# Softmax normalisation and square sums moved to GpSimd, queries split once with DMAs to place the halves, in a one-core hybrid attention and FFN block

## The chip, the core and the metric

The kernel runs on one core of a Trainium2 chip. The metric is the device time of one execution in microseconds (us), lower is better. TensorE (PE) multiplies; VectorE (DVE), ScalarE (ACT) and GpSimd (POOL) work elementwise; SyncE (SP) issues the DMAs. Each engine works through its own queue in program order, and waits on semaphores for what other engines produce.

## The reference

One layer over 512 tokens of width 2048, in fp32, cut to what matters here:

```
h    = rms_norm(x)                       # over 2048 channels: a sum of squares per token
proj = h @ w_in                          # 30 tiles of 128 columns: a q,k,v  b u,g  c q,k,v
out_a = dilated_mixture(rms(aq), rms(ak), av)      # 8 heads x 64, mixture of 3 windows
out_b = silu(layer_norm(causal_conv31(bu * sigmoid(bg))))   # 512 channels
out_c = band_attention(rms(cq), rms(ck), cv, sinks)         # 16 heads x 64, window 128
x = x + concat(out_a, out_b, out_c) @ w_out
h2 = rms_norm(x)                         # the second sum of squares
x = x + (silu(h2 @ w_gate) * (h2 @ w_up)) @ w_down          # d_ff 5632
```

In the attention, scores are shifted by their maximum, exponentiated, and divided by their sum. That division is one of the things that the change touches.

## The kernel before, in words

All arrays are held channels by tokens: a tile has 128 channels on the partitions and 512 tokens along the row. For precision every operand is split into a rounded high part (`hi`, type fp32r) and the remainder (`lo`), and each product is three matmuls, hi·hi, hi·lo and lo·hi (`mm3`, lines 248 to 251). A weight unit of 128x1024 is loaded by SP (L213), rounded by ACT (L226 or L231) and its remainder taken by DVE (L227 or L232). L232 takes the high part from a copy in PSUM, L227 from SBUF. Units are split two ahead of their use.

**Head (about 0 to 52 us).** x is loaded, scaled and split (`scaled`, L338 on ACT and L339 on DVE), and multiplied with the first four column tiles. Beside it `add_square` squares each x tile on ACT (L347) and adds it to `ssum` on DVE (L348). `token_scale` sums `ssum` over the partitions with matmuls (L289).

**Projection and attention (about 52 to 525 us).** `project` makes one tile of 128 columns from two weight units. A clock of ticks (`Ticks`, line 82) is advanced after every six matmuls. Everything else is put into the program at a set number of ticks after the tile it depends on, so the order on every engine is fixed by these numbers. After a q tile (two heads of 64 channels), `do_q` copies it to SBUF (`raw`, L471), then in the next tick takes the high part on ACT (L509), one tick later the remainder on DVE (L514), per head. For head h, the tile `q[h]` has the high part on that head's 64 partitions and the remainder on the other 64; the keys stand in both halves, so that one matmul of 128 partitions sums both products. Beside these, each of the 124 taps of the convolution (L424, L426, DVE) has a tick, and so have the keys (`do_k`, whose halves are copied across by two DMAs on SP, L546) and the values.

`attention` handles each head in units of one or two blocks of 128 queries: `scores` (PE, L615 and L616), `top` (DVE, L622: mask and maximum, reading PSUM), `exps` (ACT, L635), `norm` (DVE: the sums, L644 or L647, reciprocal, L649, and the division, L651, one instruction for each block of queries), `flip` (PE transposes of the normalised weights, L667), their split (`ph`, ACT L673; `pl`, DVE L678), `weigh` (PE, L691 and L692), and the output (`mix`, ACT L700 and DVE L705), which is split for the output projection at L736 and L737.

**Output projection (about 421 to 622 us).** Two halves of 16 units each. In the second half `residual` adds the product to x (L830, DVE), stores it, calls `add_square` for `ssum2`, and after every second tile `h2_of` makes the seven operands of a Strassen-like FFN product: two scalings on ACT (L812), four differences on DVE (L817 to L820), seven splits (L805 on ACT, L806 on DVE). From unit 88 on GpSimd adds weight blocks for the FFN (L178).

**FFN (about 622 us to the end).** Blocks of seven products each (L921). Its first block waits for `h2_of` and, for the second norm, for `ssum2`.

All 128x512 work tiles come from one pool of 75 slots, returned when the last user is done.

Of the kernel before, what the change touches and what calls it, by code (L numbers as in the profile page):

```python
# [9 lines left out]
F32 = mybir.dt.float32  # L10
F32R = mybir.dt.float32r
I32 = mybir.dt.int32
AF = mybir.ActivationFunctionType
ALU = mybir.AluOpType
# [7 lines left out]
HALF = (slice(0, HD), slice(HD, 2 * HD))  # L22
# [91 lines left out]
def kernel(ctx: ExitStack, tc: tile.TileContext, xT, wi, wo, wgu, wd, cst_in, outT):  # L114
    nc = tc.nc
# [16 lines left out]
    ticks = Ticks()  # L132

    def slot(name, dt=F32, cols=T):
        return sp.tile([P, cols], dt, name=name, tag="s")
# [203 lines left out]
        nc.vector.scalar_tensor_tensor(lo, x, g, hi.bitcast(F32), op0=ALU.mult, op1=ALU.subtract)  # L339
        return hi, lo  # L340

    def add_square(acc, x, k, tag):
        if k == 0:
            nc.scalar.activation(acc, x, AF.Square)
        else:
            sq = slot(f"{tag}{k}")
            nc.scalar.activation(sq, x, AF.Square)  # L347
            nc.vector.tensor_add(acc, acc, sq)  # L348

    def token_scale(acc, n, name, b=None):  # L350

# [9 lines left out]
    for k in range(2):  # L361
        h_hl[k] = scaled(xs[k], col(C_G1 + k), "h", k)
        split_up_to(k)
    pump(RAW_EARLY)
    add_square(ssum, xs[0], 0, "sq")
    for k in range(KT):
        if k < 2 or k % 2 == 0:
            wh, wl = next_unit()
            o = 0
        if k + X_AHEAD < KT:  # L370
            load_first(k + X_AHEAD)
        if k + 2 < KT:
            h_hl[k + 2] = scaled(xs[k + 2], col(C_G1 + k + 2), "h", k + 2)
        if k + 1 < KT:
            add_square(ssum, xs[k + 1], k + 1, "sq")
        hi, lo = h_hl.pop(k)
        h_hi.append(hi)
        h_lo.append(lo)
        for j in range(HEAD4):
            mm3(g4[j], wh[:, o:o + P], wl[:, o:o + P], hi, lo, k == 0, k == KT - 1)  # L380
            o += P
# [26 lines left out]
    hconv, yconv = {}, {}  # L408
# [22 lines left out]
    ln = {}  # L431
# [19 lines left out]
    def ln_square():  # L451
        ln["s"] = slot("lnv")
        for j in range(NB):
            add_square(ln["s"], yconv[j], j, "lq")

    def ln_var():
        ln["r"] = token_scale(ln.pop("s"), 512, "lv")[1]
# [10 lines left out]
    def head_scales(b, name, then):  # L468

        raw = slot(name + "raw")  # L470
        nc.scalar.copy(raw, b)  # L471

        def flip():
            b2 = bank(name + "f")
            for i in range(NT):
                nc.tensor.transpose(b2[:, i * P:(i + 1) * P], raw[:, i * P:(i + 1) * P], ident)
            ticks.after(1, square, b2)

        def square(b2):
            sq = slot(name + "sq")  # L480
            nc.scalar.activation(sq, b2, AF.Square)
            ticks.after(1, total, sq)

        def total(sq):
            v = cp.tile([P, NT, 2], F32, name=name + "v", tag="hsv", bufs=3)
            nc.vector.tensor_reduce(v.rearrange("p a b -> p (a b)"), sq.rearrange("p (a b) -> p a b", b=HD),
                                    axis=mybir.AxisListType.X, op=ALU.add)
            nc.vector.tensor_add(v, v, c64[:, :, None].to_broadcast([P, NT, 2]))
            ticks.after(1, power, v)

        def power(v):
            r = cp.tile([P, NT, 2], F32, name=name + "r", tag="hsr", bufs=4)
            nc.gpsimd.tensor_tensor(r, v, nhalf.rearrange("p (a b) -> p a b", b=2), op=ALU.pow)
            then(r)

        ticks.after(SQ, flip)
        return raw

    def do_q(box, b, name):
        def then(r):  # L500
            box["rq"] = r

        raw = head_scales(b, name, then)
        box["q at"] = ticks.now + SQ + 4
        q = box["q"] = [slot(f"{name}{h}", F32R) for h in range(2)]

        def high():
            for h in range(2):
                nc.scalar.copy(q[h][HALF[h]], raw[HALF[h]])  # L509
            ticks.after(1, low)  # L510

        def low():
            for h in range(2):
                nc.vector.tensor_sub(q[h][HALF[1 - h]], raw[HALF[h]], q[h][HALF[h]].bitcast(F32))  # L514
        ticks.after(1, high)

    def do_k(box, b, name, gi):
# [77 lines left out]
    def attention(kind, box, mix, mi, heads):  # L595
        ready, every, step, s1, sx, s2, fl, ev, we = C_TICKS if kind == "c" else A_TICKS
        name = mi
# [5 lines left out]
        def head(h):  # L603
            es = {}
            d = cp.tile([P, 4, NT], F32, name=f"{name}d{h}", tag="soft", bufs=6)
            mx, nm, den, rd = (d[:, i] for i in range(4))
# [33 lines left out]
            def norm(u):  # L640
                e = es[u]
                s = slice(us[u][0][0], us[u][-1][0] + 1)
                if kind == "c":
                    nc.vector.tensor_add(den[:, s], den[:, s], mx[:, s])  # L644
                else:
                    for i, k0, n, o in us[u]:
                        nc.vector.scalar_tensor_tensor(e[:, o:o + n], e[:, o:o + n], 1.0, mult_a[:, T - n:],  # L647
                                                       op0=ALU.mult, op1=ALU.mult, accum_out=den[:, i:i + 1])
                nc.vector.reciprocal(rd[:, s], den[:, s])  # L649
                for i, k0, n, o in us[u]:  # L650
                    nc.vector.tensor_scalar(e[:, o:o + n], e[:, o:o + n], rd[:, i:i + 1], None, op0=ALU.mult)  # L651

            ph, pl = {}, {}

# [21 lines left out]
            def low(t, b, o):  # L676
                pl[t] = slot(f"{name}pl{h}{t}", F32R)
                nc.vector.tensor_sub(pl[t][:, :o], b[:, :o], ph[t][:, :o].bitcast(F32))  # L678
# [36 lines left out]
            for u in range(len(us)):  # L715
                tu = t0 + u * step
                ticks.after(tu, scores, u)
                ticks.after(tu + s1, top, u)
                ticks.after(tu + s1 + sx, exps, u)
                ticks.after(tu + s1 + sx + s2, norm, u)  # L720
# [28 lines left out]
    ticks.after(t_ln + 2, ln_mean)  # L749
    ticks.after(t_ln + 4, ln_center)  # L750
    ticks.after(t_ln + 6, ln_square)
    ticks.after(t_ln + 9, ln_var)
    ticks.after(t_ln + 12, ln_out, mix)
# [4 lines left out]
    for name in PROJ[HEAD4:]:  # L758
        kind, what, j = name[0], name[1], name[2:]
        if name == PROJ[-1]:  # L760
            for n, row in enumerate(ROWS[:2]):
                ticks.after(4 + n, split_mix, row)
        b = project(name)
        if kind == "b":
            part[what + j] = b
            if what == "g":
                ticks.after(0, glu, int(j), part.pop("u" + j), part.pop("g" + j))
            continue
        if kind == "c":
            box = Heads(shared) if j else shared  # L770
        else:
            box = boxes.setdefault(j, {})
        if what == "k":
            do_k(box, b, name, 1 if kind == "c" else 0)
        elif what == "v":
            do_v(box, b, name)
        else:
            do_q(box, b, name)
        if what == "q":
            if kind == "a":  # L780
                boxes.pop(j)
            attention(kind, box, mix, kind + j, (int(j), int(j) + 8) if kind == "c" else None)
# [61 lines left out]
    for half in range(2):  # L844
        for i, n in enumerate(OUT_ORDER[half]):
# [6 lines left out]
            for kk in range(8):  # L852
                k = 8 * half + kk
# [4 lines left out]
                s = slice(kk * P, (kk + 1) * P)  # L858
# [221 lines left out]
    for g in range(2 * NP + len(DOWN)):  # L1080
# [5 lines left out]
        else:  # L1086
            n, first, end = DOWN[t]
# [116 lines left out]
```

## Time and profile before

| | before |
|---|---|
| median of 3 runs | 1931.52 us (1931.4 to 1932.05) |
| the profiled execution: span from first to last instruction | 1932.4 us |
| mean granted TensorE clock | 0.993 |
| busy, us: PE / DVE / ACT / POOL | 1899.8 / 1474.8 / 1334.0 / 993.4 |
| moved by DMA | 313.99 MB, mean 162 GB/s |

The profiled execution has no time of its own outside its span; its span stands 0.9 us above the median. How to read the rows that follow: a line number is one of the kernel's. `out<-in xcount` names tiles without buffer numbers. In the groups, "busy, mean ns" is followed by the engine's idle time before the instructions and by what ended it. In a table of windows, each row gives the stretch, its length, and the busy time (and count of instructions) of PE, PEld, DVE, ACT and POOL, then the granted clock of TensorE as a share of full speed, the DMA share and GB/s. In a timeline, the columns are start, duration, engine, line, operation, tiles, shape and count, and in brackets the idle time before it and what ended it.

### The profile page before, as it was taken

The numbers are of one execution on the slowest core, as the hardware profiler recorded it, in microseconds if no ns is written. First come the engines' busy times: TensorE is split into PE (matmuls) and PEld (weight loads), VectorE is DVE, ScalarE is ACT, GpSimd is POOL, SyncE is SP. The second block draws the span as 40 slices with busy tenths as digits, with TensorE's granted clock in tenths as the row PEclk, the third lists the DMA queues.
The fourth block names the chain that finished last, engine by engine and source line by source line (L and its number), as shares of the span: only waits on it lengthen the run. The fifth ranks groups of instructions, "written<-read, shape, count | busy, mean of one in ns | idle before, by whom it ended". The sixth has DMA issues, their size and how long they took to land.

```text
span 1932.4 us, 29509 instructions
## 1 busy us (share of the span) xinstructions
PE 1899.8 (98%) x10332; PEld 1645.2 (85%) x10332; DVE 1474.8 (76%) x2574; ACT 1334.0 (69%) x1848; POOL 993.4 (51%) x640
## 2 busy tenths in 40 slices
PE   8999999999999999999999999999999899999999
PEld 7888788778877888888888888888888788888888
DVE  6789988997468677777777777777777677767776
ACT  6355655553355788888887888888888677667675
POOL 0111011000001688877877888778887566656564
PEclk9999999989999899999999999999999999999999
DMA  7222222223332254535443444444447777777685
GB/s 263 75 99 72 66 88 77 72 87 113 122 114 93 94 184 139 174 126 178 150 167 133 165 164 159 141 159 167 159 142 259 286 275 278 269 243 272 202 276 195
DMA packets 132133, 313.99 MB, mean 162 GB/s; under 512 B 14736, under 2 KB 30224, under 8 KB 131984
## 3 DMA queue, kind: packets, MB, share of 16 engines
q1 hardware_dynamic: 131840, 312.01, 47.4%
q8 instruction: 81, 1.33, 0.3%
q14 instruction: 68, 0.56, 0.1%
q10 hardware_dynamic: 144, 0.10, 0.0%
HBM read 255.42 MB, written 55.31 MB: 161 GB/s over the span
## 4 chain that ended last, share of the span: by engine, by line
PE 70%; DMA 1%; DVE 0%; POOL 0%; ACT 0%; issue 0%; POOLq 0%; DVEq 0%
PE out L921 66%; PE o L250 1%; PE o L249 1%; PE o L251 1%; DMA w('22', 'd1')_15059<-in_wd 0%; DMA a<-od 0%; POOL w('21', 'd1')_15057 L178 0%; DVE xr L830 0%; PE out L289 0%; DVE h L806 0%; ACT sr L347 0%; ACT h L812 0%; DVE wl L232 0%; POOL w('s', 'd1')_15138 L178 0%; ACT wh L231 0%
## 5 line engine op out<-in xcount | busy, mean ns | idle before, releaser
L921 PE MATMUL out<-h,wh 128*128 128x512 f32 x2464 | 591.0, 392 | 3.6 <-DVE h L806 3.6
L921 PEld LDWEIGHTS out<-h,wh 128*128 128x128 f32 x2464 | 454.1, 189 | 91.8 <-DVE h L806 4.0
L921 PEld LDWEIGHTS out<-h,wl 128*128 128x128 f32 x2464 | 317.5, 192 | 13.8 <-ACT r2b L885 1.2
L921 PE MATMUL out<-h,wl 128*128 128x256 f32 x2464 | 321.5, 283 | 1.2 <-ACT r2b L885 0.9
L921 PE MATMUL out<-a,wh 128*128 128x512 f32 x1232 | 297.8, 392 | 4.2 <-DMA a<-od 3.0
L921 PEld LDWEIGHTS out<-a,wh 128*128 128x128 f32 x1232 | 226.0, 188 | 50.1 <-DMA a<-od 5.3
L921 PEld LDWEIGHTS out<-a,wl 128*128 128x128 f32 x1232 | 160.4, 193 | 8.1 <-DMA a<-od 1.5
L226 ACT CAST wh<-w 128x1024 fp32r<-128x1024 f32 (+1 forms) x93 | 96.8, 1040 | 99.4 <-PE o L250 33.2
L921 PE MATMUL out<-a,wl 128*128 128x256 f32 x1232 | 163.0, 284 | 0.9 <-DMA a<-od 0.9
L227 DVE TENSOR_TENSOR wl<-w,wh 128x1024 fp32r<-128x1024 f32 (+1 forms) x93 | 112.5, 1211 | 65.5 <-ACT wh L226 65.3
L934 DVE TENSOR_TENSOR y<-y,out 128x256 f32<-128x256 f32 x120 | 50.6, 421 | 64.0 <-PE out L921 60.9
L426 DVE SCALAR_TENSOR_TENSOR y<-bu,cst,y 128x511 f32<-128x511 f32 (+14 forms) x120 | 87.7, 731 | 0.7
L178 POOL TENSOR_TENSOR w('s', 'g1')_5639<-w('21', 'g1')_5403,w('22', 'g1')_5439 128x1024 f32<-128x1024 f32 x1 | 2.4, 2409 | 116.2 <-DVE wl L227 116.2
L935 DVE TENSOR_TENSOR y<-y,out 128x256 f32<-128x256 f32 x120 | 50.5, 421 | 4.1
L250 PE MATMUL o<-ml_c,wh 128*128 128x512 f32 x128 | 51.0, 398 | 2.1 <-DVE ml_c L737 2.1
L249 PE MATMUL cq<-hh,wh 128*128 128x512 f32 x128 | 51.3, 401 | 1.4 <-DVE mix_c L705 1.4
L249 PE MATMUL o<-mh_c,wh 128*128 128x512 f32 x128 | 51.7, 404 | 0.0
L251 PE MATMUL o<-mh_c,wl 128*128 128x512 f32 x128 | 50.7, 396 | 0.0
L251 PE MATMUL cq<-hh,wl 128*128 128x512 f32 x128 | 50.0, 390 | 0.0
L250 PE MATMUL cq<-hl,wh 128*128 128x512 f32 x128 | 49.9, 390 | 0.0
L249 PE MATMUL in<-hh,wh 128*128 128x512 f32 x64 | 26.3, 411 | 5.6 <-ACT wh L226 5.6
L250 PEld LDWEIGHTS o<-ml_c,wh 128*128 128x128 f32 x128 | 24.5, 191 | 7.5 <-DVE ml_c L737 3.1
(3093 smaller groups left out, 4835.4 us busy)
## 6 DMA issues: line engine op xcount, KB each, us to landing
a<-od SPq DMA_DIRECT2D x182, 256.0 KB, 5.3
od<-a SPq DMA_DIRECT2D x147, 256.0 KB, 3.8
w<-in_wi SPq DMA_DIRECT2D x59, 512.0 KB, 3.6
w<-in_wo SPq DMA_DIRECT2D x32, 512.0 KB, 3.6
y<-x2d SPq DMA_DIRECT2D x48, 256.0 KB, 5.3
x2d<-y SPq DMA_DIRECT2D x64, 128.0 KB, 3.3
x<-in_xT SPq DMA_DIRECT2D x16, 256.0 KB, 7.2
xr<-in_xT SPq DMA_DIRECT2D x16, 256.0 KB, 3.8
```

What stands on the lines that cost most here:

```text
L178: nc.gpsimd.tensor_add(out[:, :n], raws[key[a]][0][:, :n], raws[key[b]][0][:, :n])
L226: nc.scalar.copy(hi[:, :n], t[:, :n])
L227: eng.tensor_sub(lo[:, :n], t[:, :n], hi[:, :n].bitcast(F32))
L249: nc.tensor.matmul(out, wh, xh, start=start, stop=False)
L250: nc.tensor.matmul(out, wh, xl, start=False, stop=False)
L251: nc.tensor.matmul(out, wl, xh, start=False, stop=stop)
L426: nc.vector.scalar_tensor_tensor(yconv[j][:, i:], hconv[j][:, :T - i], c, yconv[j][:, i:], op0=ALU.mult, op1=ALU.add)
L921: nc.tensor.matmul(out, lhs[:, s], rhs, start=begin, stop=last and low == flip[0] and x is xs[-1], skip_group_check=True)
L934: sign(out, out if first is None else first, main)
L935: sign(out, out, rest)
```

## The change

Three edits, with nothing else moved.

```diff
-    def add_square(acc, x, k, tag):
+    def add_square(acc, x, k, tag, eng=nc.gpsimd):
         if k == 0:
             nc.scalar.activation(acc, x, AF.Square)
         else:
             sq = slot(f"{tag}{k}")
             nc.scalar.activation(sq, x, AF.Square)
-            nc.vector.tensor_add(acc, acc, sq)
+            eng.tensor_add(acc, acc, sq)
...
     def ln_square():
         ln["s"] = slot("lnv")
         for j in range(NB):
-            add_square(ln["s"], yconv[j], j, "lq")
+            add_square(ln["s"], yconv[j], j, "lq", nc.vector)
...
         def high():
+            hi = slot(f"{name}hi", F32R)
+            nc.scalar.copy(hi, raw)
+            ticks.after(1, low, hi)
+
+        def low(hi):
+            lo = slot(f"{name}lo", F32R)
+            nc.vector.tensor_sub(lo, raw, hi.bitcast(F32))
             for h in range(2):
-                nc.scalar.copy(q[h][HALF[h]], raw[HALF[h]])
-            ticks.after(1, low)
-
-        def low():
-            for h in range(2):
-                nc.vector.tensor_sub(q[h][HALF[1 - h]], raw[HALF[h]], q[h][HALF[h]].bitcast(F32))
+                nc.sync.dma_start(q[h][HALF[h]].bitcast(F32), hi[HALF[h]].bitcast(F32))
+                nc.sync.dma_start(q[h][HALF[1 - h]].bitcast(F32), lo[HALF[h]].bitcast(F32))
         ticks.after(1, high)
...
                 nc.vector.reciprocal(rd[:, s], den[:, s])
                 for i, k0, n, o in us[u]:
-                    nc.vector.tensor_scalar(e[:, o:o + n], e[:, o:o + n], rd[:, i:i + 1], None, op0=ALU.mult)
+                    nc.gpsimd.tensor_scalar(e[:, o:o + n], e[:, o:o + n], rd[:, i:i + 1], None, op0=ALU.mult)
```

In words: the additions of the squares of x and of x2 (15 each) go from DVE to GpSimd, while the layer norm's three stay on DVE. For each of the 12 q tiles, two ACT copies and two DVE subtractions of 64x512 become one of each of 128x512, into two new slots; four DMAs of 64x512 (128 KB) on SP then place the halves into `q[0]` and `q[1]`. The 96 multiplications that divide the softmax weights go from DVE to GpSimd.

## The prediction

> **What bounds the kernel now.** The head of the page comes first, then the slices.
>
> ```profile
> PE 1899.8 (98%) x10332; PEld 1645.2 (85%) x10332; DVE 1474.8 (76%) x2574; ACT 1334.0 (69%) x1848; POOL 993.4 (51%) x640
> ...
> DVE  6789988997468677777777777777777677767776
> ...
> PEclk9999999989999899999999999999999999999999
> ```
>
> TensorE is busy 98% of the span, so the change, which leaves its matmuls alone, can only fill its gaps. A slice is 48 us: DVE is at 8 or 9 tenths from slice 4 to 9 (about 145 to 480 us), the attention. In the two slices where the clock reads 8 TensorE lost speed too. Next, the waits of PE (total us, times, longest).
>
> ```profile
> PE out L921 <- DVE h L806: 3.6, 1, 3.6
> PE c2o L692 <- DVE c2pl L678: 2.6, 1, 2.6
> PE a2o L692 <- DVE a2pl L678: 2.5, 2, 2.2
> PE o L250 <- DVE ml_c L737: 2.1, 1, 2.1
> PE a0o L692 <- DVE a0pl L678: 2.1, 2, 1.9
> PE cq L249 <- DVE mix_c L705: 1.4, 1, 1.4
> ```
>
> All name DVE: five in the attention, one at the start of the FFN. The table of windows prices the stretches around them.
>
> ```profile
> 134.00:203.00 69.00, 67.62 (x368) 57.75 (x367) 65.47 (x180) 40.55 (x97) 7.32 (x4) 1.00 0.22 69
> 203.00:230.00 27.00, 24.01 (x122) 19.91 (x121) 24.51 (x63) 16.69 (x37) 3.26 (x2) 0.94 0.17 59
> 304.00:438.00 134.00, 127.33 (x638) 106.09 (x636) 128.99 (x320) 70.77 (x131) 9.71 (x5) 0.96 0.24 77
> ...
> 600.00:640.00 40.00, 36.20 (x157) 30.23 (x155) 31.59 (x58) 25.64 (x46) 7.17 (x4) 0.87 0.28 94
> ```
>
> A stretch costs TensorE its idle time, plus length times what the clock (third number from the end) lacks to 1:
> - 134 to 203: 69.00 - 67.62 = 1.4 us.
> - 203 to 230: 3.0 + 0.06 x 27 = 4.6 us.
> - 304 to 438: 6.7 + 0.04 x 134 = 12.0 us. DVE is busy 129.0 of 134 us here: it is the bound, and what is taken from it comes back nearly whole, up to 12.0.
> - 600 to 640: 3.8 + 0.13 x 40 = 9.0 us.
>
> So some 18 us can be won in the attention, and the FFN start is a place to win or lose.
>
> **What DVE gives up.**
>
> ```profile
> L651 DVE TENSOR_SCALAR a1e<-a1e,a1d 128x128 f32<-128x128 f32 (+3 forms) x8 | 2.9, 386 | 0.2
> L651 DVE TENSOR_SCALAR c6e<-c6e,c6d 128x256 f32<-128x256 f32 (+1 forms) x8 | 2.3, 334 | 0.1
> ...
> L514 DVE TENSOR_TENSOR cq<-cq7raw,cq x2: 686/688/689, 207.9 to 208.7; 64x512 fp32r<-64x512 f32 x2
> ```
>
> The divisions take 2.9 us for two `a` heads and 2.3 for two `c` heads; measured from start to the next start (DVE overlaps neighbours by about 0.08 us) 2.4 and 2.0. A q split loses one of two 0.7 us subtractions. ACT loses as much, but it is not what PE waits for: zero.
>
> **What GpSimd charges.** No row shows this multiplication on GpSimd. The nearest rows, of one input and of two:
>
> ```profile
> 1.01 0.29 POOL masks.py:199 TENSOR_SCALAR_AFFINE_SELECT ident<-ident 128x128 f32<-128x128 f32 x1
> ...
> L416 POOL TENSOR_TENSOR bu<-bu,bg 128x512 f32<-128x512 f32 x4 | 5.1, 1286 | 19.2 <-ACT bg L413 14.5 <-DVE c5d L644 4.7
> ```
>
> Scaled by columns with a fixed part of 0.13, one input gives 0.29, 0.45, 0.61 and 0.77 us for 128 to 512 columns; two inputs would give up to 1.29 for 512. I take the first, which has one tensor input as here; the second is the upper end. Below, the same as DVE is the least (0.3 us less for 512 columns).
>
> GpSimd's time would be free if it ran beside DVE. It doesn't always:
>
> ```profile
> 591.36 2.41 POOL L178 TENSOR_TENSOR w('s', 'g1')_5639<-w('21', 'g1')_5403,w('22', 'g1')_5439 128x1024 f32<-128x1024 f32 x1 [116.22 <-DVE wl L227]
> 593.84 2.72 POOL L178 TENSOR_TENSOR w('21', 'g1')_5403<-w('21', 'g1')_5403,w('11', 'g1')_5506 128x1024 f32<-128x1024 f32 x1
> ```
>
> ```profile
> 592.57 1.74 DVE L348 TENSOR_TENSOR ssum<-ssum,sr 128x512 f32<-128x512 f32 x1 [0.70 <-ACT sr L347]
> 594.23 2.61 DVE L817 TENSOR_TENSOR ta<-h 128x256 f32<-128x256 f32 x1
> 596.77 0.41 DVE L818 TENSOR_TENSOR ta<-h,h 128x256 f32<-128x256 f32 x1
> ```
>
> L817 has the size of L818, 0.41 us, but lasts 2.61, until GpSimd's second addition is over; L348, before it, ends some 0.5 us after the first one does. Both read two tensors from SBUF. The Trainium skill (SBUF — State Buffer, Who interferes with whom) has the rule: a DVE instruction with two SBUF inputs, and a GpSimd one that reads SBUF, exclude each other for a whole instruction, while one that takes an input from PSUM is free. By this rule, the trace agrees (2.61 against 0.41), the change moves less work than it seems to.
>
> I therefore went through the DVE instruction behind each division. In the 304 to 438 stretch lie 6 `a` heads (18 groups of divisions) and 2 `c` heads (4 groups). Behind 15 of the 18, the next one reads PSUM (L622, L678, L705) and lasts about as long as GpSimd needs: free. Behind 3 of 18 and 3 of 4 it is a tap, a subtraction or a weight split: GpSimd waits for it, then holds up the next for 0.6 to 0.9 us. Freed: 3 x 2.4 + 2.0 + 4 x 0.7 = 12.0; held up 6 x 0.75 = 4.5; left **7.5 us** of the 12.0 that PE loses. In 203 to 230: 0.7 for the split of q7 and three groups for 1.5, so 2.2 us; this takes the 2.6 us wait to 0.4, and a wait so short should not halve the clock, so 2.2 + 1.6 = **3.8 us**. In 134 to 203 two q splits and several free groups cover the **1.4 us**. Elsewhere in the attention PE does not wait for DVE, and what DVE gains there is idle time.
>
> GpSimd's results come later than DVE's did. Worst placed are the `a` heads:
>
> ```profile
> 378.28 0.49 DVE L651 TENSOR_SCALAR a1e<-a1e,a1d 128x512 f32<-128x512 f32 x1
> ```
>
> ```profile
> L667 PE MATMUL a1t<-ident,a1e x20: 270/272/273, 381.2 to 401.0; 128*128 128x128 f32 x20
> ```
>
> The last division ends at 378.8, the transposes start at 381.2: 2.4 us of slack. GpSimd needs 0.3 us more and up to 0.7 of waiting: hidden. Without that cover it would be 1 us per head at most.
>
> **The halves of q.** SP's transfers wait for the subtraction, and the scores for them.
>
> ```profile
> DMA to landing us min/median/max: 2.2/2.3/3.3
> ```
>
> ```profile
> 92.98 1.25 SPq L546 DMA_DIRECT2D ck<-ck  x2
> ```
>
> ```profile
> 210.11 0.33 PE L615 MATMUL c7s<-ckh,cq 128*128 128x128 f32 x1
> ```
>
> These are the key's copies of the same 128 KB: 0.6 us per issue, 2.3 to land. Head 0 needs the first two of four, and the high part's can go ahead of the remainder. In before, q7's scores start 0.7 us after its remainder (208.7 + 0.7); they are the tightest. With one subtraction fewer and 0.5 us of divisions gone, the remainder ends at 208.2 and the second DMA lands at about 210.5, 0.4 after the scores started; with the semaphores at both its ends I take **+0.7 us**. None of the other eleven q tiles is among the waits above, and their scores stand further behind: I charge nothing; at worst 0.5 for each of four (q3 of `c`, q1 to q3 of `a`), 2 us. Behind these DMAs on SP wait only weight loads, whose units are split two ahead.
>
> **The square sums.** In the head no wait of PE names DVE, and x tiles are split two ahead, which hides a hold-up of 1.3 us: zero; without that cover, up to 1.3 for each of 15. In the second half of the output projection the chain of two tiles looks like this (DVE):
>
> ```profile
> 579.17 1.23 DVE L227 TENSOR_TENSOR wl<-w,wh 128x1024 fp32r<-128x1024 f32 x1 [0.31 <-ACT wh L226]
> 580.31 0.68 DVE L830 TENSOR_TENSOR xr<-xr,o 128x512 f32<-128x512 f32 x1
> 581.70 0.69 DVE L348 TENSOR_TENSOR ssum<-ssum,sr 128x512 f32<-128x512 f32 x1 [0.70 <-ACT sr L347]
> 582.31 0.43 DVE L817 TENSOR_TENSOR ta<-h 128x256 f32<-128x256 f32 x1
> ...
> 589.05 0.69 DVE L348 TENSOR_TENSOR ssum<-ssum,sr 128x512 f32<-128x512 f32 x1 [0.70 <-ACT sr L347]
> 590.05 1.22 DVE L227 TENSOR_TENSOR wl<-w,wh 128x1024 fp32r<-128x1024 f32 x1 [0.31 <-ACT wh L226]
> ```
>
> One round takes 10.88 us with hardly a gap, as long as PE's two units. L348 is hidden: after it, L817 waits for ACT's scaling and L227 for ACT's weight copy in any case. On GpSimd the addition takes 1.29 and starts when ACT's square ends, as L348 did (2.5 us into the round), so it holds L817 up to 3.9 instead of 3.14, and the rest of the round starts 0.6 late; the second holds the next L227 for 0.35. A round grows by about 0.95, three rounds by 2.9. In the next (590 to 604) L178 is in the same queue, so that three GpSimd operations hold DVE up instead of two: 1.8; then 0.5, where weights are split from PSUM, and 0.9, beside another L178; the last gains 0.2, as two squares follow each other without an addition between. So the operands for the FFN come **5.9 us** later, behind the 3.6 us wait that is there already: it becomes 9.5. Removing DVE's additions doesn't buy that back.
>
> **The sum.** On the profiled execution: 1932.4 - 1.4 - 3.8 + 0.7 - 7.5 + 5.9 = 1926.3. Its span stands 0.9 above the median, so **1925.5 us** as a median.
>
> **The rivals.**
> 1. *The lock decides.* GpSimd's multiplication costs as much as two inputs (1.29 for 512 columns, 0.43 to 1.0 for less). Then the free places no longer cover it: the attention keeps the q splits only, about 5 us; the FFN start loses 5.9, and with a late weight split beside it and another window of half clock (0.13 x 40 us cost 5.2 before) up to 10. Sum -5 + 10, or 1931.5 + 5 = 1936.5. It decides from the point where the attention's gain falls below the FFN's loss, so if GpSimd takes about 0.8 us for 256 columns. For it: every DVE stretch here reads SBUF twice in more than half its time. Against: the free places.
> 2. *No lock worth the name*: DVE slips in ahead of GpSimd, and the additions cost nothing. -1.4 - 4.6 - 12.0 + 0.7 = -17.3: 1914.2 us. Against: the 2.61 us row.
> 3. *The wait moves to the DMAs*: q's halves land late behind weight loads, or the new slots, read by DMAs, make ACT wait for a free one. PE waits 0.5 to 1 us for each of 8 of 12 tiles, +6 on the forecast: 1931.5, no change.
> 4. *The GpSimd page's rate*: the Trainium skill (GPSIMD Engine Reference, Engine selection) calls one-input operations roughly line rate. By this page's rule the division would be cheaper than I took it. No run here shows it. As a mechanism of this kernel: with DVE's own durations on GpSimd the hold-ups shrink from 4.5 to 2.5, -2 on the sum: 1923.5, inside the forecast's range.
>
> **How the numbers follow.** Forecast (with 4) 0.46, spanning 1920 to 1930; rival 1 0.26; rival 2 0.12; rival 3 0.16. A measurement of this kernel can tell 0.2% from no change, 3.9 us: the bounds are 1927.7 and 1935.4. Of the forecast 0.40 is below and 0.06 between; rival 2 is below; a quarter of rival 3 (0.04) is below; rival 1 is above but for 0.04. So faster 0.56, same 0.22, slower 0.22. The range reaches towards rival 2 and past rival 1: **1916 to 1938**.
>
> **What would show it.** L651 should stand under POOL at about 0.45 us for 256 columns; taps and L227 should show a second, longer duration. The waits for c2pl, a0pl and a2pl should be gone or below 1 us, and the half clock near 425 with them; one on c7's scores by a DMA should be new. Between 557 and 632 L817 should show about 0.8 us beyond its 0.43, and PE's wait for h (L806) be 7 to 11 us. If that stays at 3.6, the lock term was wrong; if a2pl's wait stays, GpSimd's price was.

## The result and the profile after

The changed kernel takes **1923.26 us** in the median of four executions (1922.99 to 1923.69), beside 1931.46 us for the kernel before (1930.79 to 1932.05). The medians lie 8.2 us apart; the ratio of all executions is 0.9954, with a 95% interval of 0.9942 to 0.9966, so the change is faster by about 0.4%. The profiled execution has a span of 1921.2 us and took 1922.99 us, so 1.8 us lie around the span. One of the nine executions of the run of the additions alone, below, was in a state of its own (3807.6 us) and is left out of its figures.

The changed kernel's line numbers are larger by 3 from the q split on: L651 is now L654, L678 is L681, L817 is L820. First the head of its page and the slices.

```profile
PE 1893.5 (99%) x10332; PEld 1641.9 (85%) x10332; DVE 1436.5 (75%) x2436; ACT 1325.0 (69%) x1836; POOL 1143.4 (60%) x766
...
DVE  6788888896467677777777777777777677767776
...
PEclk9999999999999999999999999999999999999999
```

DVE's busy time fell by 38.3 us and GpSimd's grew by 150.0. Both are net of hold-ups: the 96 divisions alone took DVE 34.6 us before, and they take GpSimd 104.4, some of it waiting. No slice of the clock reads 8 any more. The waits of PE (total us, times, longest):

```profile
PE out L924 <- DVE h L809: 5.1, 1, 5.1
...
PE out L924 <- DVE wl L232: 2.6, 1, 2.6
PE o L250 <- DVE ml_c L740: 2.5, 1, 2.5
...
PE a0t L670 <- POOL a0e L654: 0.6, 1, 0.6
```

Of the five waits of the attention that the prediction listed, four are gone; the fifth, for ml_c, an operand of the output projection, grew from 2.1 to 2.5 us, and a new one of 0.6 us on a division stands beside it. The FFN start has become worse: 5.1 us for h and 2.6 for a weight remainder, where 3.6 and 0.2 stood. The same stretches as before in the table of windows:

```profile
134.00:203.00 69.00, 69.00 (x378) 59.30 (x377) 60.23 (x158) 41.29 (x98) 31.43 (x28) 1.00 0.29 85
203.00:230.00 27.00, 27.00 (x144) 22.83 (x143) 24.18 (x67) 17.63 (x40) 13.94 (x12) 1.00 0.36 98
...
304.00:438.00 134.00, 130.90 (x667) 109.97 (x665) 122.51 (x292) 67.18 (x121) 48.81 (x38) 0.99 0.33 99
```

From 134 to 230 us TensorE is without a gap and at full clock. Between 304 and 438, 3.1 us idle and 1% of the clock are left.

The windows have the same clock times, but not quite the same work. What a change did to each stage is better read from one and the same matmul in two traces. These rows are from the timeline of PE in the kernel after; L289 is the first of the sums for the second norm.

```profile
183.09 0.39 PE L249 MATMUL cq<-hh,wh 128*128 128x512 f32 x1
...
222.90 0.40 PE L249 MATMUL ak<-hh,wh 128*128 128x512 f32 x1
...
270.74 0.60 PE L537 MATMUL ak0t<-ident,ak0wide 128*128 128x128 f32 x4
...
420.66 0.60 PE L476 MATMUL aq3f<-ident,aq3raw 128*128 128x128 f32 x4
...
622.50 1.70 PE L289 MATMUL out<-ones,ssum 128*128 128x1 f32 x8
```

| start of, us | cq7 (L249) | ak2 (L249) | ak0t | aq3f | L289 | last matmul |
|---|---|---|---|---|---|---|
| before | 184.91 | 229.73 | 278.27 | 434.41 | 632.56 | 1928.26 |
| after | 183.09 | 222.90 | 270.74 | 420.66 | 622.50 | 1917.03 |
| shift | -1.8 | -6.8 | -7.5 | **-13.8** | **-10.1** | -11.2 |

So 13.8 us are won up to the end of the attention (0.3 of them in the head, before 76 us), and 3.7 are lost again up to the norm's sums. Such a shift is uncertain by a us or two, since the head differs and half clock comes and goes between executions: the run of reordering alone, below, has the program of before up to 250 us, and yet reaches ak2 2.4 us earlier, 1.1 us of it since the head and the rest without the half clock near 227.

### The profile page after: what moved, and what is told of

The parts are those of the page before. It is cut to its first block, busy times and chain, and to the rows that moved or that the text cites. A ratio compares the mean times of both kernels' runs of the same rounds, so it can differ in the third digit from the quotient of the medians.

```text
span 1921.2 us, 29755 instructions
## 1 busy us (share of the span) xinstructions
PE 1893.5 (99%) x10332; PEld 1641.9 (85%) x10332; DVE 1436.5 (75%) x2436; ACT 1325.0 (69%) x1836; POOL 1143.4 (60%) x766
## 4 chain that ended last, share of the span: by engine, by line
PE 69%; DVE 1%; DMA 1%; ACT 0%; issue 0%; POOL 0%; DVEq 0%; SPq 0%; POOLq 0%; ACTq 0%
PE out L924 66%; PE o L250 1%; PE o L249 1%; PE o L251 1%; DMA a<-od 1%; DMA od<-a 0%; DMA w('22', 'd1')_15107<-in_wd 0%; DVE tb L822 0%; DVE xr L833 0%; DVE h L809 0%; ACT h L815 0%; DVE ta L821 0%; DVE wl L232 0%; DVE wl L227 0%; POOL w('21', 'd1')_15105 L178 0%
## 5 line engine op out<-in xcount | busy, mean ns | idle before, releaser
L227 DVE TENSOR_TENSOR wl<-w,wh 128x1024 fp32r<-128x1024 f32 (+1 forms) x93 | 115.0, 1238 | 93.0 <-ACT wh L226 91.2
L226 ACT CAST wh<-w 128x1024 fp32r<-128x1024 f32 (+1 forms) x93 | 96.8, 1041 | 104.4 <-PE o L250 30.5
L348 POOL TENSOR_TENSOR ssum<-ssum,sr 128x512 f32<-128x512 f32 x15 | 19.6, 1308 | 110.2 <-ACT sr L347 110.1
L249 PE MATMUL o<-mh_c,wh 128*128 128x512 f32 x128 | 51.3, 401 | 0.0
L249 PE MATMUL cq<-hh,wh 128*128 128x512 f32 x128 | 51.2, 400 | 0.0
L348 POOL TENSOR_TENSOR ssum<-ssum,sq 128x512 f32<-128x512 f32 x15 | 25.1, 1672 | 22.6 <-ACT sq L347 22.1
L654 POOL TENSOR_SCALAR a3e<-a3e,a3d 128x128 f32<-128x128 f32 (+3 forms) x8 | 11.0, 1384 | 35.8 <-DVE a3d L652 29.5
```

What stands on the lines that cost most here:

```text
L226: nc.scalar.copy(hi[:, :n], t[:, :n])
L227: eng.tensor_sub(lo[:, :n], t[:, :n], hi[:, :n].bitcast(F32))
L249: nc.tensor.matmul(out, wh, xh, start=start, stop=False)
L348: eng.tensor_add(acc, acc, sq)
L654: nc.gpsimd.tensor_scalar(e[:, o:o + n], e[:, o:o + n], rd[:, i:i + 1], None, op0=ALU.mult)
```

## The experiments

All ratios are to the kernel before, timed beside each run on the same chip, with a 95% interval. The first four runs, the next four and the last three were on three chips, where the kernel before took 1931.57, 1932.15 and 1932.39 us in the median; between these sets a difference of 1 us says nothing.

**The three parts alone.** The first leaves of the diff only its last hunk:

```diff
-                    nc.vector.tensor_scalar(e[:, o:o + n], e[:, o:o + n], rd[:, i:i + 1], None, op0=ALU.mult)
+                    nc.gpsimd.tensor_scalar(e[:, o:o + n], e[:, o:o + n], rd[:, i:i + 1], None, op0=ALU.mult)
```

> Only the 96 multiplications go to GpSimd; q split and square sums are as before. Theory: the attention is bound by DVE in 304 to 438 us, and what GpSimd takes there comes back: 9.2 of the 12.0 us freed are these multiplications, so most of the attention's gain (12 to 14 us at the end of the attention in the trace of the change) is theirs. Expected about 8 us below the kernel before, 1923.5, with the FFN start as before (PE's wait for h near 3.6). Rival: the division only moves DVE's wait to the lock, and the gain is the q split's; then under 3 us, 1928.5 or more.

Measured: 1920.07 us, 0.9937 (0.9924 to 0.9951). The divisions alone beat the whole change, and lie 3.4 us below what I expected of them; 13.5 us are won up to aq3f and kept at the FFN start (13.6 at L289). The rival is out.

The second moves only the additions of squares:

```diff
-    def add_square(acc, x, k, tag):
+    def add_square(acc, x, k, tag, eng=nc.gpsimd):
...
-            nc.vector.tensor_add(acc, acc, sq)
+            eng.tensor_add(acc, acc, sq)
...
-            add_square(ln["s"], yconv[j], j, "lq")
+            add_square(ln["s"], yconv[j], j, "lq", nc.vector)
```

> Only the 30 additions of squares go to GpSimd. Theory: L817 and L227 are held in each round of the second half of the output projection by about 0.6 and 0.3 us, so the operands of the FFN come 3 to 6 us later: 1935 to 1937, and no gain in the head. Rival: the additions cost nothing beside the rounds, and the longer wait for h in the change comes from the earlier end of the attention: then 1931.5, no change.

Measured: 1.0027 (1.0017 to 1.0037), eight executions between 1934.8 and 1940.0 us, 1937.65 in the mean, 0.6 above the theory's range. The trace loses nothing up to aq3f (-0.3) and is 4.1 us late at L289. In its waits the one for h has kept its length, and a second one, for the remainder of a weight, stands beside it:

```profile
PE out L921 <- DVE h L806: 3.5, 1, 3.5
...
PE out L921 <- DVE wl L232: 2.5, 1, 2.5
```

The theory's mechanism is confirmed, though not the wait that I had in mind: DVE's chain of the last round but one ends 2.6 us late, and PE meets this at the weight remainder (L232) that stands behind the operands in DVE's order; the last round's operands come 4 us late, but PE is late by then too. Beyond the 2.5 us wait, some 1.5 us of the 4.1 are half clock, which starts earlier there (627 us). In the head the additions hold DVE too, but mostly beside cover: in the trace of the change L339 takes 1328 ns in the mean there instead of 748, and no wait of PE names it. In two other traces with these additions one does, for 0.3 us (this run) and 0.9 us (the last but one below).

```profile
L339 DVE SCALAR_TENSOR_TENSOR hl<-x,cst,hh 128x512 fp32r<-128x512 f32 x16 | 20.8, 1328 | 3.7 <-ACT hh L338 3.7
```

The third makes only the q split with its DMAs:

```diff
-                nc.scalar.copy(q[h][HALF[h]], raw[HALF[h]])
...
-                nc.vector.tensor_sub(q[h][HALF[1 - h]], raw[HALF[h]], q[h][HALF[h]].bitcast(F32))
...
+            nc.scalar.copy(hi, raw)
...
+            nc.vector.tensor_sub(lo, raw, hi.bitcast(F32))
             for h in range(2):
+                nc.sync.dma_start(q[h][HALF[h]].bitcast(F32), hi[HALF[h]].bitcast(F32))
+                nc.sync.dma_start(q[h][HALF[1 - h]].bitcast(F32), lo[HALF[h]].bitcast(F32))
```

> Only the q split with its DMAs; divisions and square sums stay on DVE. Theory: DVE loses 0.7 us for each of 12 q tiles, 2.8 us of it in 304 to 438 and 0.7 ahead of the 2.6 us wait at 226; about 3.5 us below the kernel before, 1928, and no wait of PE for a DMA of q. Rival (the split is what gains): 6 us or more below, 1925.5. Other rival (the DMAs cost what the split saves): 1931.5.

Measured: 1924.83 us, 0.9964 (0.9952 to 0.9977): 6.7 us, where the theory had 3.5. By size the first rival came. No wait of PE names a DMA of q, but one is close: PE is idle for 0.8 us before c7's scores, put down to DVE's c2d, which ended at 209.14 us; q7's second DMA landed at 209.07, so it would have held the scores nearly as long. The windows show where the rest of the gain came from:

```profile
203.00:230.00 27.00, 25.56 (x137) 21.40 (x136) 25.03 (x73) 15.83 (x36) 3.60 (x2) 1.00 0.36 98
298.00:430.00 132.00, 126.24 (x644) 105.81 (x643) 126.14 (x316) 68.42 (x128) 9.72 (x5) 0.99 0.32 94
```

DVE is still busy 126 of 132 us, but the clock is at 1.00 and 0.99 instead of 0.94 and 0.96. The trace's record of the granted clock has 3.4 us of half speed near 424 instead of 10.2, and none near 227. At half speed each of these windows costs half its length, so 3.4 + 1.7 = 5.1 of the 8.0 us won up to aq3f are clock, and only some 3 are shorter waits. By themselves the divisions won 11.5 us and the q split 6.7; the next run has both (and the additions of x on GpSimd) and wins 12.3: they remove the same waits.

**The additions for the second norm.** The change, but with these on DVE:

```diff
-        add_square(ssum2, t, n, "sr")
+        add_square(ssum2, t, n, "sr", nc.vector)
```

> The change, but the 15 additions for the second norm (ssum2) stay on DVE; those of x stay on GpSimd. Theory: the FFN start's loss of about 4 us in the trace of the change (h waits 5.1, the weight split 2.6) goes away: 1919.5, faster than both kernels. Rival: the loss there comes from the attention's earlier end, which leaves DVE less time ahead of the FFN, and not from the additions: 1923.

Measured: 1919.30 us, 0.9933 (0.9921 to 0.9945), faster than the change by 4.0. PE's wait for h is 3.6 us again, and the shift at aq3f (-14.9) is kept at L289 (-15.2). The rival is out: the loss is the additions'.

**What holds DVE.** The divisions alone on GpSimd, but with the reciprocal as a second tensor operand:

```diff
-                    nc.gpsimd.tensor_scalar(e[:, o:o + n], e[:, o:o + n], rd[:, i:i + 1], None, op0=ALU.mult)
+                    nc.gpsimd.tensor_mul(e[:, o:o + n], e[:, o:o + n], rd[:, i:i + 1].to_broadcast([P, n]))
```

> The 96 multiplications alone on GpSimd (as in the run of that edit alone, 1920.1 us), but with the reciprocal spread as a second tensor operand. Theory, from the trace of the change: GpSimd's one-input multiplication holds VectorE only for a small part of its time (0.2 to 0.4 us of 0.92 to 1.57), its two-input addition for all of it (L817 1.07 instead of 0.43). Then the two-input form holds the next DVE instruction with two SBUF operands 0.4 to 1.0 us in about a third of the 96 places: 5 to 8 us more in DVE's durations in the attention, 2 to 5 us slower than the one-input form, 1922 to 1925. Rival: GpSimd waits for DVE in either form, and only the latency differs: 1919 to 1921.

Measured: 1922.54 us, 0.9951 (0.9938 to 0.9963), 2.5 us slower than the one-input form, as the theory had it. The two intervals touch, but the traces show the same 2.5 us at aq3f (420.90 and 423.45 us). The group of one tile's two heads, in the kernel after (first) and in this run (shortest, median and longest ns):

```profile
L654 POOL TENSOR_SCALAR c4e<-c4e,c4d x8: 611/924/1569, 262.3 to 275.9; 128x256 f32<-128x256 f32 x6, 128x128 f32<-128x128 f32 x2
```

```profile
L651 POOL TENSOR_TENSOR c4e<-c4e,c4d x8: 400/614/1594, 264.6 to 278.3; 128x256 f32<-128x256 f32 x6, 128x128 f32<-128x128 f32 x2
```

The form with two tensors is the *quicker* one on GpSimd: 400 and 614 ns for 128 and 256 columns, against 611 and 924. And yet the kernel is slower, because DVE pays. Matched by name, shape and order, 743 DVE instructions that start between 134 and 545 us in the trace of before last 13.0 us longer in this run, and 4.3 us longer with the one-input form. Most of the difference is in two small instructions of the softmax, L625 (+5.6 against -0.6 us) and L644 (+2.4 against +0.2). One group of the first (the divisions alone, then this run):

```profile
L625 DVE SCALAR_TENSOR_TENSOR a1d<-a1d,aq1r x6: 159/160/164, 354.8 to 375.8; 128x1 f32<-128x1 f32 x4, 128x2 f32<-128x2 f32 x2
```

```profile
L625 DVE SCALAR_TENSOR_TENSOR a1d<-a1d,aq1r x6: 159/287/447, 356.9 to 377.8; 128x1 f32<-128x1 f32 x4, 128x2 f32<-128x2 f32 x2
```

**Order.** What was left in the attention was the wait for ml_c, though the row that it belongs to (c2) was complete from about 237 us. So the next run splits the first two rows of the output projection where DVE has time; its base is the run with ssum2 on DVE:

```diff
+        if name == "ak0":
+            for n, row in enumerate(ROWS[:2]):
+                ticks.after(4 + n, split_mix, row)
         if name == PROJ[-1]:
-            for n, row in enumerate(ROWS[:2]):
+            for n, row in enumerate(ROWS[2:4]):
                 ticks.after(4 + n, split_mix, row)
```

> The change with ssum2 on DVE (1919.3 us), and the splits of the first two rows of the output projection (L736, L737) moved from 405 to about 250 us, rows 2 and 3 to where those stood. Theory: what is left in 304 to 438 is one wait of 2.5 us for ml_c and the 3.4 us at half clock behind it, 4.2 us together; DVE is 1.2 us freer there, and rows 2 and 3 no longer come from behind L647 and L227, so the wait goes below 1 us and the half clock with it: 1915 to 1916.5. Rival: DVE's queue is as long as before at this place, and the wait moves to another operand (a2pl, a later ml_c): 1918.5 to 1919.5.

Measured: 1918.31 us, 0.9929 (0.9917 to 0.9942): 1.0 us below its base, which the intervals do not tell from none, so closer to the rival. The wait did move, but not to an operand of DVE's:

```profile
PE a2t L670 <- POOL a2e L654: 2.5, 1, 2.5
```

```profile
413.87 2.43 POOL L654 TENSOR_SCALAR a2e<-a2e,a2d 128x512 f32<-128x512 f32 x1 [3.30 <-PE a2t L670]
```

The next thing late is GpSimd's own latency. The half clock behind the wait is gone. From 405 to 425 us, without the early split (first) and with it:

```profile
405.00:425.00 20.00, 17.52 (x84) 14.30 (x83) 19.90 (x37) 14.06 (x27) 5.10 (x3) 0.91 0.41 119
```

```profile
405.00:425.00 20.00, 17.33 (x89) 14.07 (x88) 19.90 (x38) 12.84 (x25) 6.01 (x3) 1.00 0.41 119
```

A wait of the same 2.5 us stands there in both (PE, without the early split and with it):

```profile
415.73 0.50 PE L250 MATMUL o<-ml_c,wh 128*128 128x512 f32 x1 [2.48 <-DVE ml_c L740]
```

```profile
416.36 0.33 PE L670 MATMUL a2t<-ident,a2e 128*128 128x128 f32 x1 [2.52 <-POOL a2e L654]
```

What decides between them is where the wait falls. In every trace here the record of the granted clock changes on a grid of 3.41 us: its stretches of half clock last one, two or three steps (3.41, 6.83, 10.24 us), and those of full clock between them whole numbers of steps too. Without the early split the wait lies inside one step, from 412.8 to 416.3 us, and half clock follows from 416.3. With it, the grid (counted back from the next change, at 613.3) has a boundary at 415.3, which cuts the wait into 1.5 and 1.0 us, and nothing follows. I counted PE's idle time in each step at full clock of all 13 traces from 20 to 1400 us: 26 steps have 1.8 us or more of it, and half clock follows on 25 of them; all others have at most 1.52, and it follows on none. This is a count of what the traces have, not an experiment that moved a wait against the grid; behind 1400 us some steps with 1.3 to 1.5 us were followed by half clock as well. How many steps it lasts stays open.

The next run puts the squares of x2 behind the operands of the FFN, on the same base:

```diff
+        if n < NJ:
+            return
+        pair = [(k, x2[k]) for k in (n - NJ, n)]
-        add_square(ssum2, t, n, "sr", nc.vector)
-        if n >= NJ:
-            h2_of(n - NJ)
+        h2_of(n - NJ)
+        for k, t in pair:
+            add_square(ssum2, t, k, "sr", nc.vector)
```

> The change with ssum2 on DVE (1919.3 us), and in the second half of the output projection both squares of a pair come after h2_of instead of before it. Theory: in the last round two ACT squares and the waits of DVE for them (about 1.4 us each) stand ahead of the operands of the FFN; without them PE's wait for h falls from 3.6 to about 2 us and the half clock behind it gets shorter: 1915 to 1917.5. Rival: the sum for the second norm comes later and PE waits for it, or ACT's order loses elsewhere what is won: 1919 to 1921.

Measured: 1915.88 us, 0.9912 (0.9897 to 0.9927), 3.4 us below its base (4.1 by the ratios). The wait for h is gone from the list; part of the rival holds too, as the norm's sums now wait:

```profile
PE out L289 <- DVE ssum L348: 2.0, 1, 2.0
```

Both edits together:

> Both edits of the two runs before this one. Theory: they act at different places (410 and 610 us) and add up: 1911 to 1914. Rival: as one of the two alone, 1915 to 1919.

Measured: 1915.68 us, 0.9914 (0.9901 to 0.9928), between 1913.1 and 1917.5. That is no more than the second edit alone, so the rival; in the profiled execution they did add up (16.9 us at aq3f, 19.7 at L289, half clock for 3.4 us only), but that was the quickest of its executions.

Two more on this base. In the first, divisions of 512 columns stay on DVE:

```diff
+                    eng = nc.gpsimd if n < 512 else nc.vector
-                    nc.gpsimd.tensor_scalar(e[:, o:o + n], e[:, o:o + n], rd[:, i:i + 1], None, op0=ALU.mult)
+                    eng.tensor_scalar(e[:, o:o + n], e[:, o:o + n], rd[:, i:i + 1], None, op0=ALU.mult)
```

> As the run with both reorderings (1915.7 us, of 1913.1 to 1917.5), but the 8 multiplications of 512 columns go back to DVE, the other 88 stay on GpSimd. Theory: the last wait in the attention there, 2.5 us for a2e, is GpSimd's latency (2.43 us for 512 columns, behind DVE's L227 and L737); DVE does it in 0.48 and 2 us earlier, so the wait goes below 1 us; elsewhere DVE has 0.4 us more per instruction, three of them in 304 to 438: 1.5 to 2.5 us below, 1913 to 1914.5. Rival: the wait goes back to ml_c or a2pl, as DVE is the bound again: 1915 to 1917.

Measured: 1915.40 us, 0.9910 (0.9895 to 0.9925), in the rival's range. The wait for a2e, DVE's now, has shrunk to 0.5 us and 0.8 us more is won up to aq3f, but in the time the difference cannot be told. With DVE earlier, a DMA of q is what PE waits for, for the first time:

```profile
PE a3s L618 <- DMA aq<-aq3lo: 0.7, 1, 0.7
```

The second also moves the squares between the second and the third operand:

```diff
-        h = []
+        h, pair = [], [(k, x2[k]) for k in (j, j + NJ)]
...
-        for q, src in ((5, n1), (1, h11), (7, n3), (6, n2), (2, h21), (4, n4), (3, h22)):
+        for i, (q, src) in enumerate(((5, n1), (1, h11), (7, n3), (6, n2), (2, h21), (4, n4), (3, h22))):
+            if i == 2:
+                for k, t in pair:
+                    add_square(ssum2, t, k, "sr", nc.vector)
             operand(q, j, src)
...
-        pair = [(k, x2[k]) for k in (n - NJ, n)]
         h2_of(n - NJ)
-        for k, t in pair:
-            add_square(ssum2, t, k, "sr", nc.vector)
```

> As the run just before it, but each pair of squares comes after the second of the seven operands of h2_of instead of after the last. Theory: PE's wait for h stays away (the first two operands are what it asks for first) and the 2.0 us wait of L289 for ssum falls below 0.5: 1.5 us below that run, 1911.5 to 1913. Rival: the third operand (h of product 7) comes 1.4 us later and PE waits for it instead: no gain, 1913 to 1914.5.

Measured: 1914.66 us, 0.9904 (0.9890 to 0.9917), the lowest time of all, though its interval overlaps those of the three runs before it; it lies just above the rival's range. In the trace the theory's waits did go: L289's for ssum fell from 2.0 to 0.3 us, h does not come back, and there is no half clock at the FFN start. The list of waits has no entry over 1.1 us in the attention or at the FFN start:

```profile
PE o L250 <- DVE ml_c L741: 1.1, 3, 0.6
PE o L250 <- DVE ml_b L741: 1.1, 2, 0.8
PE out L931 <- ACT r2b L895: 0.9, 1, 0.9
```

Last, order alone: the kernel before with the early split and the squares after h2_of, and nothing on GpSimd.

```diff
+        if name == "ak0":
+            for n, row in enumerate(ROWS[:2]):
+                ticks.after(4 + n, split_mix, row)
...
-        add_square(ssum2, t, n, "sr")
-        if n >= NJ:
-            h2_of(n - NJ)
+        if n < NJ:
+            return
+        pair = [(k, x2[k]) for k in (n - NJ, n)]
+        h2_of(n - NJ)
+        for k, t in pair:
+            add_square(ssum2, t, k, "sr")
```

> The kernel before, with nothing moved to GpSimd and no change of q, but the two reorderings (two rows of the output projection split at 250 us, squares of x2 after h2_of). It asks whether order alone would have done. Theory: the FFN start gains its 3 to 4 us as before, but DVE has no more time in the attention than its 1.2 us, and the waits for c2pl, a0pl and a2pl with their half clock stay: 1926 to 1928. Rival: the waits of the attention were a matter of order too: 1922 or less.

Measured: 1925.54 us, 0.9962 (0.9950 to 0.9975). It is half a us below the theory's range; the half clock near 425 got shorter (6.8 us instead of 10.2), against the theory. The waits for c2pl (2.6), a2pl (3.0) and a0pl (2.0) stay, as the theory said: order moves what is late, but the attention needs DVE's time.

## Why the prediction was right, point by point

The forecast of 1925.5 us lies 2.2 above the measured time, and its mechanism was the one found: DVE gives the attention back its gaps, and the square sums cost some of that at the FFN start. Several terms had the wrong size, though, and they offset each other in part, so that the closeness of the number is in part luck. (Two slips on which nothing hangs: 1926.3 less 0.9 is 1925.4, and the slices of 8 or 9 tenths of DVE are 3 to 9, about 97 to 435 us.)

**134 to 203 us (-1.4) and 203 to 230 (-3.8, with +0.7 for q7's DMAs).** Measured -1.8, then -5.0. The DMAs' term (+0.7) was zero: no wait of PE names one of them in the kernel after, though q7's second DMA landed at 207.81 us, only 0.16 before the scores start. The clock went to 1.00, as foreseen, but these 1.6 us were not safe to count. An identical program up to 250 us (the run of order alone) had the same wait of 2.6 us without the half clock: the grid cut it into 1.5 and 1.1 us, where before 2.5 us of it lay in one step.

**GpSimd's price.** I took 0.29 to 0.77 us for 128 to 512 columns from the masking row, and called two inputs (1.29 for 512) the upper end. The rows have 0.60, 0.92, 1.25 and 1.57 at the least: twice what I took, and above that end. Rival 1 was to decide from about 0.8 us for 256 columns. That point was passed, and the rival still did not come, because the other factor, what a GpSimd instruction does to DVE, was wrong by more.

**The hold-up of DVE (6 x 0.75 = 4.5 us in 304 to 438).** This is the step that failed most. In the kernel after, 280 matched DVE instructions there last only 1.8 us longer in sum. The number of places was about right (8 are longer by over 0.1 us), but each is held for 0.27 us in the mean, not 0.75. The rule that I took from the Trainium skill (SBUF — State Buffer, Who interferes with whom), exclusion for a whole instruction, fits the additions, and does not fit the division: the trace agrees for one and not for the other. One place shows it, first GpSimd, then DVE:

```profile
415.43 2.87 POOL L654 TENSOR_SCALAR a2e<-a2e,a2d 128x512 f32<-128x512 f32 x1 [3.38 <-DVE a2d L652]
```

```profile
415.13 1.22 DVE L227 TENSOR_TENSOR wl<-w,wh 128x1024 fp32r<-128x1024 f32 x1
416.27 1.70 DVE L740 TENSOR_TENSOR ml_c<-mix_c,mh_c 128x512 fp32r<-128x512 f32 x2
417.89 0.71 DVE L426 SCALAR_TENSOR_TENSOR y<-bu,cst,y 128x485 f32<-128x485 f32 x1
```

GpSimd starts while L227 runs and lasts 1.30 us longer than the shortest of its kind (1.57): by this, it is GpSimd that waits. DVE then loses 0.4 us, once (two L740 took 1.29 before), and its next tap runs at its usual 0.71 while GpSimd still has 0.4 us to go. That one place shows how; that it is so in general rests on the sums. With two tensor inputs the hold-up was about what I had assumed: 5.5 us in this stretch in the run with that form, by the same matching.

**What came back (-7.5 of 12.0 in 304 to 438).** Measured -6.2 from ak0t to aq3f. The forecast is near, for another reason than mine: DVE got almost all the freed time, but PE caught up with the next thing in DVE's order, ml_c (2.5 us, and the half clock behind it shrank from 10.2 to 3.4 us instead of going), and with GpSimd's latency, which I had taken for hidden (0.6 us for a0e). That these errors cancel is luck.

**The FFN start (+5.9).** Measured +3.7 to L289. The lock is there: L820 takes 1.00 to 1.08 us instead of 0.43, and L227 1.54 instead of 1.22, each held until about the end of GpSimd's addition (first GpSimd, then DVE).

```profile
565.41 1.29 POOL L348 TENSOR_TENSOR ssum<-ssum,sr 128x512 f32<-128x512 f32 x1 [6.42 <-ACT sr L347]
569.19 1.30 POOL L348 TENSOR_TENSOR ssum<-ssum,sr 128x512 f32<-128x512 f32 x1 [2.49 <-ACT sr L347]
```

```profile
558.19 1.08 DVE L820 TENSOR_TENSOR ta<-h 128x256 f32<-128x256 f32 x1 [1.31 <-ACT h L815]
...
566.25 1.54 DVE L227 TENSOR_TENSOR wl<-w,wh 128x1024 fp32r<-128x1024 f32 x1 [1.64 <-ACT wh L226]
...
569.77 1.00 DVE L820 TENSOR_TENSOR ta<-h 128x256 f32<-128x256 f32 x1 [1.38 <-ACT h L815]
```

I had 0.8 for L817 and 0.35 for L227, and a round growing by 0.95; the starts of L820 at 558.19 and 569.77 make a round of 11.6 us, 0.7 more than 10.88. A round that grows less, and two waits (h 5.1, wl 2.6) in place of one of 9.5, are the 2.2 us that I charged too much. Undoing these additions gave 4.0 us back.

**Span and median.** The forecast for the span was 1926.3; it came to 1921.2, 5.1 less: about 1.8 in the attention, 2.2 at the FFN start and 1.1 behind it. That the time was missed by only 2.2 has a further cause. I set the span of before 0.9 above the median. In the later runs 1.7 to 2.1 us lie around the span, most often 1.8, so that execution took about 1934.2 us and stood 2.7 above the median of 1931.52. Part of what its trace showed as lost is not lost in a median execution. By how much that helped the forecast is luck.

**What would have shown it.** The waits for c2pl, a0pl and a2pl are gone, as foreseen; the half clock near 425 shrank; the new wait on c7's scores did not come; the price under POOL was double (0.92 us for 256 columns, not 0.45). L817 was 0.6 us longer, where I had 0.8, and PE's wait for h came to 5.1 us, below the 7 to 11 that I named.

## What to carry to other kernels

Price a move to GpSimd by two numbers, its own duration and what its operand form takes from DVE beside it; here the form that was quicker on GpSimd made the kernel slower, and the slower one cost DVE a third as much (4.3 us against 13.0). Gaps that one queue leaves are not additive: divisions (11.5 us) and q split (6.7) gave 12.3 together, since they end the same waits, and then the next operand in the order is late. So take the moves whose cover holds (divisions in the attention), keep at home those that sit on a serial chain (the sums before the FFN), and look at the order of what comes last; that brought 1914.66 us here, against 1923.26.

## What was not expected of the hardware

- On GpSimd, a multiplication by a value per partition took 0.60 and 0.92 us for 128 and 256 columns, one of the same size with two tensor operands 0.40 and 0.61; for 512 it was 1.57 against 1.04.
- Beside the first, 743 DVE instructions lasted 4.3 us longer in sum, beside the second 13.0 us.
- The granted clock falls to half for 3.4, 6.8 or 10.2 us behind waits of PE of some 2 to 5 us, in steps of a grid of 3.41 us. Up to 1400 us it followed on 25 of the 26 steps with 1.8 us or more of idle time of PE, and on no other, so the same wait of 2.5 us came with half clock where it lay inside a step and without it where a boundary cut it. Shorter waits removed some of these windows: 5.1 us of the q split's gain.
